# Hybrid decoder trunk: the order of the seven block products ahead of a norm, and the slot of the final norm's row

## The chip, the cores and the metric

The kernel runs on one core of one Trainium2 chip. The time is the device time of one execution in microseconds (us). All matrix products run on TensorE (PE), and the instructions of each engine run in the order in which a planner has put them.

## What is computed

The reference is two layers of a decoder trunk on 512 rows of 1024 numbers in float32. In each layer three branches (a state space scan, latent attention, a gated delta rule) read the normalised rows; their gated sum `mixed` passes through an output projection and a feed-forward block:

```python
xn = rmsnorm(x, norm1_g)
...
h = x + mixed @ w_out
f = jnp.square(jax.nn.relu(rmsnorm(h, norm2_g) @ w_up)) @ w_down
x = h + f
...
return rmsnorm(x, final_norm_g)
```

The change bears on `mixed @ w_out`, on `@ w_down`, and on the norms that follow them: `norm2` after the first, the next layer's `norm1` after the second in layer 0, the final norm after the second in layer 1.

## The kernel before

**Three matmuls for one.** Each float32 operand is split into a high and a low part (`split_half` L149 for weights, with the cast to `whi` on ScalarE, ACT, L154, and the difference `wlo` on VectorE, DVE, L155). `mm3` (L180) issues three matmuls, whose lines are L182, L183 and L184.

**Seven products for eight.** `seven` (L1123) multiplies a 512-row operand by a 1024 x 1024 block of weights with a scheme that forms sums of blocks first. The result has four quarters: row half i (rows 0 to 255 are half 0) and column half j. The seven products are named a11, a12, s1, s2, s3, s4 and a22; each is 24 matmuls, over four pieces of weights (k) and two row tiles (t). Their PSUM banks: `x` (two banks, one per row tile) gathers a11, then s2, s3 and a22 on top of it; `z` (two banks) takes s1, then s4 on top; a12 has banks of its own (`sm`). After each product its banks are added to, or subtracted from, a quarter of `h` by DVE (L1145): a11 and a12 make quarter (0,0), s2 and s4 make (0,1), s1 and s3 make (1,1), a22 makes (1,0). So half 0 is final after a12 and s4, half 1 after s3 and a22. Where a norm follows (`sq` is given), the sum of squares of each final piece is taken on ACT (L1147, L271), and a22 finishes row tile 0 before row tile 1.

The order of the seven products is written out by hand (L1163 to L1181): a11, a12, s2, s1, s3, s4, `before_last`, a22. Between them stand `plus4` (L1169, the weights of a22: DVE, two pieces) and the weights of s2, the two `halves`, which DVE adds at L1160 into slots of the pool tag "f".

**Three places use the hook `before_last`.** After `w_out` (both layers, L1255) it starts `norm2` for half 0 (`n2(0)`). After the last of the four blocks (`qd == 3`) of `w_down` in layer 0 it writes rows of half 0 to DRAM (`finish`, L1271) and starts the next layer's `norm1` for half 0. In layer 1 it does the final norm of half 0 and writes the output (L1268, L1269). `norm_half` (L279) adds the two sums of squares (L275), raises them to a power on GpSimd (L259), scales each row tile (DVE L285, 128x1024, into a tile of tag "f" or "xr"), transposes 16 blocks on PE into three `sm` banks, four blocks to a bank (L290), and splits each result into `xh` and `xl` (`split_gain`, ACT L254 and DVE L255). Half 1 follows inside the next projection, which works on half 0 alone first.

**Forms.** In the `w_out` product the left operands of the seven products are formed from `mixed` just ahead of each product (`forms` L1225, `form` L1230, by way of `pre`): a `comb` is one DVE instruction (L1217), a `put` one ACT (L1212) and one DVE instruction (L1213), each on 128x256 and four of them (d) to a product. In this order s2's step makes two combs and a put for each d, s1's step a put for s1, a comb and a put for s4. In the `w_down` products the operands are formed earlier, in `up`.

**What sets the order.** The planner simulates the kernel with a cost model of its own and puts on each engine, whenever that is free, the ready instruction of the highest priority; priority is the order of the program text, apart from blocks under `tc.high_priority()`. A pool tag has a fixed number of slots; a tile that asks for a slot waits until the earlier tile's readers are done. In `ends` (L1329) of layer 1 the row of the final norm `gb` asks for a slot of "f" (four slots, used just before by the four blocks f of `up`) and is loaded by DMA from SyncE's queue (SP), ahead of the two `halves` of `seven`.

Of the kernel before, what the change touches and what calls it, by code (L numbers as in the profile page):

```python
# [10 lines left out]
F32 = mybir.dt.float32  # L11
# [4 lines left out]
ALU = mybir.AluOpType  # L16
# [4 lines left out]
P = 128  # L21
S = 512
T = S // P
D = 1024
# [31 lines left out]
def hybrid_kernel(ctx, tc, a, out, depth=2, taps=None):  # L56
    nc = tc.nc
    pe, act, dve, pool, sync = nc.tensor, nc.scalar, nc.vector, nc.gpsimd, nc.sync
    uid = itertools.count()

    def mk(pl, shape, dt, tag, bufs=None):
        return pl.tile(shape, dt, tag=tag, name=f"{tag}_{next(uid)}", bufs=bufs)
# [269 lines left out]
    ssq = []  # L332
# [18 lines left out]
    for ly in range(depth):  # L351
# [198 lines left out]
        for hp in range(4):  # L550
# [37 lines left out]
            qd = mk(lp, [P, S], F32, "mix", 8)  # L588
# [29 lines left out]
            for j in range(2):  # L618
# [3 lines left out]
                for t in range(T):  # L622
# [10 lines left out]
                    n = (t + 1) * P  # L633
# [486 lines left out]

            return b, after

        def seven(pl, ops, b, sq=None, before_last=None, fin=None, nf=4, pre=None, mid=None):  # L1123

            x, z = ([acc_bank() for _ in range(2)] for _ in range(2))

            def product(ps, n, raw, start, i, j, op, done):

                w = []
                if pre:  # L1130
                    pre(n)
                for k in range(4):
                    w.append(split_half(raw(k)))
                    if done == 2 and sq:
                        continue
                    for t in range(2):
                        mul(ps, n, w, k, t, start)
                for t in range(2):
                    if done == 2 and sq:
                        for k in range(4):  # L1140
                            mul(ps, n, w, k, t, start)
                    r = 2 * i + t
                    hs_ = h[:, r, j * 512 : (j + 1) * 512]
                    with tc.high_priority():
                        dve.tensor_tensor(hs_, hs_, ps[t], op)  # L1145
                    if done and sq:
                        square(sq[r][:, j : j + 1], hs_, pl, "fs", 3 if nf == 4 else 2)  # L1147
                        if done == 2 and fin:
                            fin(r)

            def mul(ps, n, w, k, t, start):
                ah, al = (o[:, k % 2 * 256 + t * P : k % 2 * 256 + (t + 1) * P] for o in ops[n][k // 2])
                mm3(ps[t], ah, al, *w[k], start and k == 0, k == 3, not start)

            b11, p3, b21, b22, p1 = (b[n] for n in ((0, 0), (0, 1), (1, 0), (1, 1), "p1"))

            halves = [mk(pl, [P, 2 * S], F32, "f", nf) for _ in range(2)]
            for q, o in enumerate(halves):
                cs = slice(q * 1024, (q + 1) * 1024)
                dve.tensor_tensor(o, p1[:, cs], b22[:, cs], ALU.add)  # L1160
            p2 = lambda k: halves[k // 2][:, k % 2 * 512 : k % 2 * 512 + 512]
            of = lambda o: lambda k: o[:, k * 512 : (k + 1) * 512]
            product(x, "a11", of(b11), True, 0, 0, ALU.add, 0)  # L1163
            if mid:
                mid()
            product([sm_bank() for _ in range(2)], "a12", of(b21), True, 0, 0, ALU.add, 1)
            p4 = mk(pl, [P, 4 * 512], F32, "wr00") if mid else p1

            def plus4(q):  # L1169
                cs = slice(q * 1024, (q + 1) * 1024)  # L1170
                dve.tensor_tensor(p4[:, cs], halves[q], b21[:, cs], ALU.add)

            product(x, "s2", p2, False, 0, 1, ALU.subtract, 0)
            product(z, "s1", of(p1), True, 1, 1, ALU.add, 0)
            plus4(0)
            product(x, "s3", of(p3), False, 1, 1, ALU.subtract, 1)
            plus4(1)
            product(z, "s4", of(b22), False, 0, 1, ALU.add, 1)
            if before_last:
                before_last()  # L1180
            product(x, "a22", of(p4), False, 1, 0, ALU.add, 2)  # L1181

        with tc.tile_pool(name="wo", bufs=1, reuse_waits="tile") as wo:
            slots = {(1, 0): (wo, "wr11"), (1, 1): (hpl, "h"), (2, 0): (wo, "wr10"), (2, 1): (wo, "fs"),
                     (3, 0): (wo, "fs"), (3, 1): (wo, "fs")}

            def gate_tile(dp, j):
                pl, tag = slots[dp, j]
                return mk(pl, [P, S], F32, tag, 2 if tag == "fs" else 1)

            out_proj(a["w_gdn_out"][ly], 2, *yg, wo, (1, 2), make=gate_tile)
            h = mk(hpl, [P, T, D], F32, "h")
            for t in range(T):
                sync.dma_start(h[:, t, :], xsrc[t * P : (t + 1) * P, :])
            hts = [h[:, t] for t in range(T)]
            b, after = seven_weights(wo, a["w_out"][ly], 0)
            for c in range(4):
                after(c)
            ops = {}
            ck_pair = lambda: list(zip(*hilo_tags(lp, "ck", 2)))  # L1200
            ops["a11"], ops["s3"] = ck_pair(), list(zip(*hilo_tags(wo, "s3", 2)))

            def mid():
                out_proj(a["w_gdn_out"][ly], 2, *yg, wo, (3,), make=gate_tile, gate_banks=lambda: [sm_bank() for _ in range(2)])
                fh, fl = hilo_tags(lp, "x")
                for i, n in enumerate(("a12", "s2", "s1", "s4")):
                    ops[n] = [(fh[2 * i + e], fl[2 * i + e]) for e in range(2)]
                ops["a22"] = ck_pair()

            def put(n, d, s):  # L1210
                hi, lo = (x[:, d % 2 * 256 : d % 2 * 256 + 256] for x in ops[n][d // 2])
                act.mul(hi, s, 0.5)  # L1212
                dve.scalar_tensor_tensor(lo, s, 0.5, f32(hi), ALU.mult, ALU.subtract)  # L1213

            def comb(x, y, op):
                s = mk(wo, [P, 256], F32, "fc", 8)
                dve.tensor_tensor(s, x, y, op)  # L1217
                return s

            half = lambda i: lambda d: mixed[d][:, HALVES[i]]  # L1220
            t0, t1 = half(0), half(1)

            held = []

            def forms(n):  # L1225
                for d in range(4):
                    with tc.high_priority() if d > 1 and n in ("a12", "s2") else nullcontext():
                        form(n, d)

            def form(n, d):  # L1230
                if n == "a11":
                    put("a11", d, t0(d))
                    put("s3", d, comb(t0(d), t1(d), ALU.subtract))
                if n == "a12":
                    put("a12", d, t0(d + 4))
                if n == "s2":
                    s = comb(t1(d), t1(d + 4), ALU.subtract)
                    s2 = comb(s, t0(d), ALU.subtract)
                    put("s2", d, s2)
                    held.append((s, s2))  # L1240
                if n == "s1":
                    s, s2 = held[d]
                    put("s1", d, s)
                    put("s4", d, comb(t0(d + 4), s2, ALU.add))
                if n == "a22":
                    put("a22", d, t1(d + 4))

            nf = []

            def n2(i, pl, *tag):  # L1250
                if not nf:
                    nf.extend(hilo_tags(lp, "x"))
                norm_half(i, hts, ssq, lambda k: col(g_n2 + k), pl, *nf, *tag)

            seven(wo, ops, b, ssq, lambda: n2(0, wo, "f", 2), nf=2, pre=forms, mid=mid)  # L1255
            xh, xl = nf
        h_ssq = [mk(sp, [P, 2], F32, "nss", 4) for _ in range(T)]
        if not last:
# [14 lines left out]
        with tc.tile_pool(name="ff", bufs=1, reuse_waits="tile") as fp:  # L1273
# [55 lines left out]
            def ends(qd):  # L1329

                if qd < 3:
                    return None, None, None
                gb = None
                if last:
                    gb = mk(fp, [P, D], F32, "f", 4)
                    sync.dma_start(gb, a["final_norm_g"].partition_broadcast(P))
                fin = lambda r: finish(r, gb)

                def before_last():
                    for t in range(2):  # L1340
                        fin(t)
                    if not last:
                        norm_half(0, hts, h_ssq, lambda k: params[0][:, 124 + k : 125 + k], fp, *nx, "f", 4)

                return h_ssq, before_last, fin

            for qd in range(4):
                b, after = down_weights(qd)
                ops = up(qd, after)
                if qd == 3 and not last:  # L1350
                    nx = hilo_tags(lp, "x")
                seven(fp, ops, b, *ends(qd))
        if not last:
            xpl = h_pool.enter_context(tc.tile_pool(name="xp", bufs=1, reuse_waits="tile"))
            xt, ssq, xsrc = h, h_ssq, hd
# [39 lines left out]
```

## Time and profile before

| what | us |
|---|---|
| median of 3 runs | 2314.41 |
| lowest and highest of them | 2310.45 and 2318.05 |
| the profiled execution, its own time | 2314.88 |
| its span in the profile | 2313.1 |
| PE busy in the span | 2272.7 |
| DVE busy in the span | 1647.6 |
| ACT busy in the span | 1200.5 |

Times in the profile's rows count from the start of the span. A row of the timeline has the start, the duration, engine, line, operation, the tile written and the tiles read, the shape, the count of merged instructions, and in square brackets how long the engine stood idle ahead of it and whose end it waited for. PE's matmuls overlap one another and their ends are modelled, so the time from one start to the next says more of PE's pace than a duration.

### The profile page before, as it was taken

Reading aid. Unit: us, or ns where it says so; the run is one execution under the profiler, and the core shown is the slowest. Engines: PE = TensorE matmul, PEld = TensorE weight load, DVE = VectorE, ACT = ScalarE, POOL = GpSimd, SP = SyncE. Lnnn points to the kernel's source line nnn. Section 1 sums busy time; section 2 is a strip of 40 time slices with the busy share of each in tenths; the row PEclk is TensorE's granted clock in tenths of the full one; section 3 lists DMA queues with packets and bytes.
Section 4 is the critical chain, followed back from the end, with each engine's and each line's share of the span. In section 5 each row is a group of like instructions: output and inputs, shape, how many; then the busy total and the mean of one; then the engine's idle time right before and its main releaser. Section 6 shows DMA issues by size and latency. Waiting matters only on the chain.

```text
span 2313.1 us, 32290 instructions
## 1 busy us (share of the span) xinstructions
PE 2272.7 (98%) x11810; PEld 1866.7 (81%) x11810; DVE 1647.6 (71%) x3256; ACT 1200.5 (52%) x2509; POOL 59.5 (3%) x74
## 2 busy tenths in 40 slices
PE   9999999999999999999999999999999999999998
PEld 8788787878887888888888887878788878888886
DVE  7777566876667768767867775668657668778668
ACT  6766644333443455554657666433334435645545
POOL 0000000000000000000000000000000000000000
PEclk9999999999999999999999999999999999999999
DMA  4223534452324243233122236334422241433231
GB/s 142 80 74 101 191 101 119 125 140 74 87 69 164 65 146 107 94 104 108 59 89 79 75 107 197 95 112 141 119 82 83 65 164 55 160 107 101 89 110 46
DMA packets 220032, 244.16 MB, mean 106 GB/s; under 512 B 34256, under 2 KB 172384, under 8 KB 219872
## 3 DMA queue, kind: packets, MB, share of 16 engines
q1 hardware_dynamic: 219872, 242.09, 34.1%
q8 instruction: 93, 1.52, 0.3%
q14 instruction: 67, 0.55, 0.1%
HBM read 225.60 MB, written 11.74 MB: 103 GB/s over the span
## 4 chain that ended last, share of the span: by engine, by line
PE 86%; DVE 8%; ACT 2%; DMA 2%; POOL 1%; issue 1%; SPq 0%; DVEq 0%; POOLq 0%; ACTq 0%
PE acc L182 22%; PE acc L183 21%; PE acc L184 21%; PE sm L184 2%; PE sm L183 2%; PE sm L182 2%; DVE wlo L155 2%; PE sm L752 1%; ACT whi L154 1%; DVE tok L880 1%; PE sm L650 1%; DVE gQ L879 1%; PE sm L1037 1%; POOL gms L259 1%; PE yt L666 1%
## 5 line engine op out<-in xcount | busy, mean ns | idle before, releaser
L155 DVE TENSOR_TENSOR wlo<-wraw,whi 128x512 fp32r<-128x512 f32 (+1 forms) x536 | 366.4, 687 | 345.7 <-ACT whi L154 337.8
L154 ACT CAST whi<-wraw 128x512 fp32r<-128x512 f32 (+1 forms) x536 | 330.1, 618 | 541.5 <-PE acc L183 374.4
L182 PE MATMUL acc<-xh,whi 128*128 128x512 f32 (+1 forms) x1344 | 522.3, 390 | 0.8 <-ACT xh L254 0.8
L184 PE MATMUL acc<-xh,wlo 128*128 128x512 f32 (+1 forms) x1344 | 522.9, 389 | 0.0
L183 PE MATMUL acc<-xl,whi 128*128 128x512 f32 (+1 forms) x1344 | 522.2, 389 | 0.3 <-DVE xl L255 0.3
L183 PEld LDWEIGHTS acc<-xl,whi 128*128 128x128 f32 x1344 | 253.0, 188 | 48.7 <-DVE xl L255 1.4
L182 PEld LDWEIGHTS acc<-xh,whi 128*128 128x128 f32 x1344 | 252.4, 188 | 49.1 <-ACT xh L254 1.5
L184 PEld LDWEIGHTS acc<-xh,wlo 128*128 128x128 f32 x1344 | 253.0, 188 | 47.5
L154 ACT CAST whi<-wr 128x512 fp32r<-128x512 f32 x168 | 104.3, 621 | 108.7 <-PE acc L183 47.7
L183 PE MATMUL acc<-yl,whi 128*128 128x512 f32 x384 | 151.6, 395 | 0.0
L182 PE MATMUL acc<-yh,whi 128*128 128x512 f32 x384 | 150.9, 396 | 0.0
L184 PE MATMUL acc<-yh,wlo 128*128 128x512 f32 x384 | 150.1, 391 | 0.0
L155 DVE TENSOR_TENSOR wlo<-wr,whi 128x512 fp32r<-128x512 f32 x168 | 113.7, 689 | 38.1 <-ACT whi L154 37.4
L691 DVE SCALAR_TENSOR_TENSOR ckl<-acc,pc,ckl 128x511 f32<-128x511 f32 (+2 forms) x168 | 120.4, 744 | 15.5 <-ACT ckl L687 8.2
L182 PEld LDWEIGHTS acc<-yh,whi 128*128 128x128 f32 x384 | 71.7, 188 | 16.0 <-ACT yh L254 1.7
L184 PEld LDWEIGHTS acc<-yh,wlo 128*128 128x128 f32 x384 | 72.2, 188 | 14.5
L183 PEld LDWEIGHTS acc<-yl,whi 128*128 128x128 f32 x384 | 72.3, 188 | 13.8
L183 PE MATMUL acc<-wlo,xh 128*128 128x512 f32 (+1 forms) x208 | 80.1, 385 | 0.0
L184 PE MATMUL acc<-whi,xl 128*128 128x512 f32 (+1 forms) x208 | 79.7, 384 | 0.0
L182 PE MATMUL acc<-whi,xh 128*128 128x512 f32 (+1 forms) x208 | 79.2, 382 | 0.0
L1145 DVE TENSOR_TENSOR h<-h,acc 128x512 f32<-128x512 f32 x120 | 77.2, 682 | 0.2 <-PE acc L184 0.2
L454 ACT ACTIVATE eE<-eE,cum 128x128 f32<-128x128 f32 x192 | 63.1, 390 | 24.5 <-DMA eE<-d_c 19.8
(453 smaller groups left out, 4557.2 us busy)
## 6 DMA issues: line engine op xcount, KB each, us to landing
wraw<-in_w_in_dram SPq DMA_DIRECT2D x144, 512.0 KB, 3.6
wraw<-in_w_up_dram SPq DMA_DIRECT2D x64, 512.0 KB, 3.6
wr<-in_w_down_dram SPq DMA_DIRECT2D x32, 1024.0 KB, 5.5
eE<-d_c SPq DMA_DIRECT2D x48, 256.0 KB, 4.2
wraw<-in_w_mla_out_dram SPq DMA_DIRECT2D x16, 512.0 KB, 3.4
eE<-d_e SPq DMA_DIRECT2D x32, 256.0 KB, 2.9
wraw<-in_w_ssd_out_dram SPq DMA_DIRECT2D x16, 512.0 KB, 3.3
wraw<-in_w_gdn_out_dram SPq DMA_DIRECT2D x16, 512.0 KB, 3.3
```

The source lines that it names most:

```text
L154: act.copy(hi, raw)
L155: dve.tensor_tensor(lo, raw, f32(hi), ALU.subtract)
L182: pe.matmul(o, ah, bh, start=start, stop=False, skip_group_check=more)
L183: pe.matmul(o, ah, bl, start=False, stop=False, skip_group_check=more)
L184: pe.matmul(o, al, bh, start=False, stop=stop, skip_group_check=more)
L259: pool.tensor_tensor(o, o, (exp if exp is not None else nhalf)[:, : o.shape[1]], ALU.pow)
L454: act.activation(o[:, i], o[:, i], AF.Relu, scale=-1.0, bias=cum[:, t, h0 + i : h0 + i + 1])
L650: pe.transpose(ps[:, n : n + P], pn[t][:, kb * P : (kb + 1) * P], ident)
L666: pe.matmul(o, v_h, th[:, c : c + w], start=kb == 0, stop=False)
L691: dve.scalar_tensor_tensor(acc[:, d:], ps[:, : S - d], taps_[3 - d], acc[:, d:], ALU.mult, ALU.add)
L752: pe.matmul(py[64 * i : 64 * i + 64, c * P : (c + 1) * P], xd[:, t, h * 64 : (h + 1) * 64], e2[h // 4][:, h % 4, :], start=True, stop=True)
L1145: dve.tensor_tensor(hs_, hs_, ps[t], op)
```

## The change

In `seven` a flag `early` gives the order a11, a12, s1, s2, s4, s3, `before_last`, a22, so that half 0 is final after the fifth product. It is set for the `w_out` products of both layers and for the last `w_down` product of layer 0; the other products keep their order. The steps of `form` follow: s1's step now makes one comb and the put of s1, s2's step one comb and its put, s4's step one comb and its put, and the raised priority for d of 2 and 3 passes from s2 to s1. `plus4` follows s2 and s4 in the new order. In layer 1 the final norm's row is allocated and loaded in a hook `prep`, behind the two `halves`.

```diff
-        def seven(pl, ops, b, sq=None, before_last=None, fin=None, nf=4, pre=None, mid=None):
+        def seven(pl, ops, b, sq=None, before_last=None, fin=None, nf=4, pre=None, mid=None, prep=None, early=False):
...
                 dve.tensor_tensor(o, p1[:, cs], b22[:, cs], ALU.add)
+            if prep:
+                prep()
...
-            product(x, "s2", p2, False, 0, 1, ALU.subtract, 0)
-            product(z, "s1", of(p1), True, 1, 1, ALU.add, 0)
-            plus4(0)
-            product(x, "s3", of(p3), False, 1, 1, ALU.subtract, 1)
-            plus4(1)
-            product(z, "s4", of(b22), False, 0, 1, ALU.add, 1)
+            later = [lambda: plus4(0), lambda: plus4(1)]
+            for n in ("s1", "s2", "s4", "s3") if early else ("s2", "s1", "s3", "s4"):
+                if n == "s1":
+                    product(z, n, of(p1), True, 1, 1, ALU.add, 0)
+                if n == "s2":
+                    product(x, n, p2, False, 0, 1, ALU.subtract, 0)
+                if n == "s3":
+                    product(x, n, of(p3), False, 1, 1, ALU.subtract, 1)
+                if n == "s4":
+                    product(z, n, of(b22), False, 0, 1, ALU.add, 1)
+                if later and n in ("s2" if early else "s1", "s4" if early else "s3"):
+                    later.pop(0)()
...
-                    with tc.high_priority() if d > 1 and n in ("a12", "s2") else nullcontext():
+                    with tc.high_priority() if d > 1 and n in ("a12", "s1") else nullcontext():
...
+                if n == "s1":
+                    held.append(comb(t1(d), t1(d + 4), ALU.subtract))
+                    put("s1", d, held[d])
                 if n == "s2":
-                    s = comb(t1(d), t1(d + 4), ALU.subtract)
-                    s2 = comb(s, t0(d), ALU.subtract)
-                    put("s2", d, s2)
-                    held.append((s, s2))
-                if n == "s1":
-                    s, s2 = held[d]
-                    put("s1", d, s)
-                    put("s4", d, comb(t0(d + 4), s2, ALU.add))
+                    held[d] = comb(held[d], t0(d), ALU.subtract)
+                    put("s2", d, held[d])
+                if n == "s4":
+                    put("s4", d, comb(t0(d + 4), held[d], ALU.add))
...
-            seven(wo, ops, b, ssq, lambda: n2(0, wo, "f", 2), nf=2, pre=forms, mid=mid)
+            seven(wo, ops, b, ssq, lambda: n2(0, wo, "f", 2), nf=2, pre=forms, mid=mid, early=True)
...
-                gb = None
-                if last:
-                    gb = mk(fp, [P, D], F32, "f", 4)
-                    sync.dma_start(gb, a["final_norm_g"].partition_broadcast(P))
-                fin = lambda r: finish(r, gb)
+                gb = []
+
+                def prep():
+                    if last:
+                        gb.append(mk(fp, [P, D], F32, "f", 4))
+                        sync.dma_start(gb[0], a["final_norm_g"].partition_broadcast(P))
+
+                fin = lambda r: finish(r, gb and gb[0])
...
-                return h_ssq, before_last, fin
+                return dict(sq=h_ssq, before_last=before_last, fin=fin, prep=prep, early=not last)
...
-                seven(fp, ops, b, *ends(qd))
+                seven(fp, ops, b, **ends(qd))
```

More of the change, by code (lines that the diff above doesn't have):

```diff
@@ L1331, in ends @@
                 if qd < 3:
-                    return None, None, None
-                gb = None
-                if last:
-                    gb = mk(fp, [P, D], F32, "f", 4)
-                    sync.dma_start(gb, a["final_norm_g"].partition_broadcast(P))
-                fin = lambda r: finish(r, gb)
+                    return {}
+                gb = []
[4 more added lines that the diff above has]
+                fin = lambda r: finish(r, gb and gb[0])
                 def before_last():
```

## Prediction

> **What bounds the kernel now.** I read the page's busy times first, then the chain that ended last, then PE's busy time in the four stretches that the change touches.
>
> ```profile
> span 2313.1 us, 32290 instructions
> ...
> PE 2272.7 (98%) x11810; PEld 1866.7 (81%) x11810; DVE 1647.6 (71%) x3256; ACT 1200.5 (52%) x2509; POOL 59.5 (3%) x74
> ...
> PE 86%; DVE 8%; ACT 2%; DMA 2%; POOL 1%; issue 1%; SPq 0%; DVEq 0%; POOLq 0%; ACTq 0%
> ```
>
> PE is busy for 2272.7 of 2313.1 us and holds 86% of the chain: the kernel is as long as PE's stream of matmuls and its gaps. All gaps together are 40.4 us, so a change that adds and removes no matmul can win only from these, and only where it touches them.
>
> ```profile
> core 0: us, PE busy (x) PEld busy (x) DVE busy (x) ACT busy (x) POOL busy (x), PEclk, DMA share, GB/s
> 815.00:831.00 16.00, 14.17 (x89) 11.92 (x88) 13.20 (x30) 8.51 (x21) 2.48 (x4) 1.00 0.42 143
> 1150.00:1166.00 16.00, 14.97 (x86) 13.17 (x86) 12.51 (x30) 8.10 (x21) 3.04 (x6) 1.00 0.56 198
> 1961.00:1977.00 16.00, 14.18 (x88) 11.88 (x87) 13.33 (x30) 8.60 (x22) 2.48 (x4) 1.00 0.40 135
> 2270.00:2285.00 15.00, 13.71 (x60) 10.73 (x59) 14.09 (x22) 8.21 (x16) 0.00 (x0) 1.00 0.00 1
> ```
>
> The second column is the length of the stretch, the third PE's busy time in it. The first and third stretch are a22 and the norm behind `w_out` in the two layers: PE idles 1.83 and 1.82 us. The second is the same place behind `w_down` in layer 0: 1.03 us. The fourth holds the third product of the last `w_down` in layer 1: 1.29 us. That is 5.97 us of idle, about a seventh of all that PE has. The granted clock is 1.00 in all four, so they differ from the rest by waits alone.
>
> PE's timeline of the first stretch shows the waits one by one.
>
> ```profile
> 809.88 0.39 PE L182 MATMUL acc<-whi,xh 128*128 128x512 f32 x1
> ...
> 815.32 0.39 PE L182 MATMUL acc<-whi,ckh 128*128 128x512 f32 x1
> ...
> 818.29 0.40 PE L183 MATMUL acc<-wlo,ckh 128*128 128x512 f32 x1
> 819.09 0.55 PE L290 MATMUL sm<-ct,f 128*128 128x128 f32 x3 [0.40 <-DVE f L285]
> ...
> 820.41 1.15 PE L290 MATMUL sm<-ct,f 128*128 128x128 f32 x9
> ...
> 824.04 0.51 PE L182 MATMUL acc<-xh,whi 128*128 128x256 f32 x2 [0.38 <-ACT xh L254]
> 825.42 0.63 PE L290 MATMUL sm<-ct,f 128*128 128x128 f32 x4 [0.88 <-DVE xl L255]
> ...
> 829.95 0.39 PE L183 MATMUL acc<-xl,whi 128*128 128x256 f32 x1 [0.17 <-DVE xl L255]
> 831.25 1.47 PE L290 MATMUL sm<-ct,f 128*128 128x128 f32 x12
> ```
>
> s4 runs from 809.88 to 815.32, so a product of 24 matmuls takes 5.44 us and a matmul's slot 0.227 us. Then a22 starts, and the planner puts half 0's transposes (L290) into it, where it thought the scaled rows `f` ready; they came 0.40 us later, and the in-order PE waited with a22's matmuls behind. The rest follows from the same lateness: the up projection waits 0.38 us for `xh`, the fourth group of transposes 0.88 us for a bank that `split_gain` (L255) still reads, a last matmul 0.17 us for `xl`. From 818.29 to 819.09 are 0.80 us between starts where a slot is 0.227: this stall cost 0.57, not 0.40, as modelled ends hide a part. So idle time is a lower bound of the loss, and each stall hides up to 0.17 us more.
>
> ```profile
> 1154.11 0.55 PE L290 MATMUL sm<-ct,f 128*128 128x128 f32 x3 [0.50 <-DVE f L285]
> ...
> 1160.10 0.63 PE L290 MATMUL sm<-ct,f 128*128 128x128 f32 x4 [0.53 <-DVE xl L255]
> ```
>
> In layer 0's `w_down` these two are all of the 1.03 us.
>
> **The change part by part.** No matmul, transpose, split or DMA is added or removed in the three places: per `w_out` four combs of s1, four of s2, four of s4 and four puts each stay, only ordered otherwise. What counts is when they come.
>
> *Half 0 a product earlier.* The chain from s4's end to the scaled rows is read on DVE.
>
> ```profile
> 815.47 1.28 DVE L1145 TENSOR_TENSOR h<-h,acc 128x512 f32<-128x512 f32 x2
> ...
> 818.28 0.75 DVE L285 TENSOR_SCALAR f<-h,nrs 128x1024 f32<-128x1024 f32 x1 [0.32 <-POOL nrs L259]
> 818.95 0.68 DVE L1145 TENSOR_TENSOR h<-h,acc 128x512 f32<-128x512 f32 x1
> 819.55 0.75 DVE L285 TENSOR_SCALAR f<-h,nrs 128x1024 f32<-128x1024 f32 x1
> ```
>
> The first scaled tile is there at 819.03, 3.7 us after s4's end, the second at 820.30, 5.0 us after. With s3 between s4 and a22, a22 starts 5.44 us after s4's end, so both come 0.4 to 1.7 us ahead of it, even with the add at 818.95 in between, which moves away. What moves in are splits of s3's and a22's weights, high priority and 0.69 us each, two more than here; that can take the second tile to 0.3 us after a22's start, with eight transposes of the first tile to do until then. In program order the transposes stand behind all of s3, so PE takes them at the seam of s3 and a22, and the lateness of 0.40 that the planner didn't foresee falls into the margin. Then `xh` and `xl` of half 0 are made during a22's 5.44 us, and the waits of 0.38 and 0.17 in the up projection go too. Won: up to 1.83 and 1.82 us of idle in `w_out`, 1.03 in `w_down`.
>
> *What is late next.* Two things, which I price per place. First, s3 and a22 now follow each other on the same banks `x`. Before, z's or a12's product always stood between two products on a bank. a22's first matmul must wait until DVE has subtracted s3's result from `h`. In the rows above the seam is at 815.32, and the add of row tile 0 starts at 815.47 and takes 0.68 us (the single add at 818.95): it ends at 816.15, some 0.8 us after the seam. The 12 transposes that three banks hold take PE longer than that (1.15 us for 9, 1.47 for 12) and stand just there. With the cover it costs nothing, without it 0.8 us; I take 0.2. Second, the fourth group of transposes still waits for a bank of `sm`; it now falls into a22, where the planner again puts it by its own estimate. Between nothing and the 0.88 us of before I take 0.25. So 0.45 us per place stay, 1.35 in all.
>
> The Trainium skill speaks against this neighbourhood ("PSUM — Partial Sum Buffer", section "PSUM bank collisions raise a hardware error"): "Semaphore-guard PSUM by bank × quadrant". By that rule no matmul may enter `x` while DVE reads it, and no cover inside the bank is possible; the trace agrees so far that a bank's reader and PE never overlap in the rows above, and no run here shows the pair s3 and a22. Where the transposes stand elsewhere, this is the first rival below.
>
> *The forms.* DVE is nearly full when they are made.
>
> ```profile
> 785.00:805.00 20.00, 20.00 (x89) 16.22 (x88) 18.88 (x38) 12.71 (x29) 0.00 (x0) 1.00 0.01 2
> ...
> 807.36 0.42 DVE L1213 SCALAR_TENSOR_TENSOR xl<-fc,xh 128x256 fp32r<-128x256 f32 x1
> ```
>
> 18.88 of 20 us are busy, PE 20.00: DVE has just been fast enough. The row at 807.36 is the last low part of s4, done at 807.78. s4 now starts where s3 did, at 809.88 − 5.44 = 804.44, and needs it for its fourth piece of weights, three quarters of a product later, at 808.5. Even at the old pace that is 0.7 us early, and the third product's forms have become fewer (one comb instead of two). Cost: 0, bounded by the third rival's price.
>
> *The other moves.* `plus4` in `w_out` runs long before (its inputs are ready), in `w_down` beside PE. The write of half 0's rows to DRAM moves a product earlier on SP's queue:
>
> ```profile
> 1151.14 3.85 SPq L1271 DMA_DIRECT2D hd<-h  x3
> 1156.87 0.38 SPq L161 DMA_DIRECT2D wraw<-in_w_in_dram  x1
> ```
>
> The next load behind it comes at 1156.87 and has no earlier one to delay; cost 0. If that cover were gone, three issues within 3.85 us would be the most.
>
> *The final norm's row.* DVE's and SP's rows show the wait.
>
> ```profile
> 2259.11 0.34 SPq L1336 DMA_DIRECT2D f<-in_final_norm_g_dram  x1
> ...
> 2277.03 1.23 DVE L1160 TENSOR_TENSOR f<-wp,wr 128x1024 f32<-128x1024 f32 x1
> ...
> 2277.33 0.39 PE L184 MATMUL acc<-whi,mix 128*128 128x512 f32 x1
> 2279.01 0.73 PE L182 MATMUL acc<-whi,mix 128*128 128x512 f32 x2 [1.29 <-ACT whi L154]
> 2279.74 0.50 PE L183 MATMUL acc<-wlo,mix 128*128 128x512 f32 x1
> ...
> 2301.48 0.75 DVE L1268 SCALAR_TENSOR_TENSOR h<-h,nrs,f 128x512 f32<-128x512 f32 x1 [0.39 <-POOL nrs L259]
> ```
>
> The row took the slot that came free first; the second of the `halves` had to wait for a block f of the last part of `up` and ran at 2277.03 to 2278.26, in the middle of s2, which reads it. The cast behind it came late and PE lost 1.29 us of idle; by starts (1.68 − 0.227) + (0.73 − 0.454) = 1.73 us. In layer 0, where no such row is loaded, the same product is the control:
>
> ```profile
> 1116.05 2.35 DVE L1160 TENSOR_TENSOR f<-wp,wr 128x1024 f32<-128x1024 f32 x2
> ...
> 1116.00:1136.00 20.00, 20.00 (x90) 16.41 (x88) 19.26 (x32) 14.83 (x28) 0.00 (x0) 1.00 0.00 1
> ```
>
> Both halves are added together, ahead of a11, and PE is busy for 20.00 of 20 us. So this stall goes whole. The row's load then waits for the last blocks f, about 2275, and is first read at 2301.48, 26 us later, with an otherwise empty queue. PE's last matmul and the tail behind it move up with it.
>
> **The sum.** Idle removed: 1.83 + 1.82 + 1.03 + 1.29 = 5.97. Hidden by modelled ends: twelve stalls (four, four, two, two) at 0 to 0.17, I take 0.1: 1.2. Given back: 1.35. Net 5.97 + 1.2 − 1.35 = 5.8 us. From the profiled execution's 2314.88 that gives **2309.1 us**; against the median 2314.41, 0.5 us lower, it is 0.23% faster. The most that can go is 5.97 + 12 × 0.17 = 8.0; the least, with only the last term (1.29) and the seam uncovered three times (2.4), is a loss of 1.1.
>
> **The rivals.**
>
> *The wait is only moved.* The planner's transposes stand inside s3 or a22 instead of the seam, so that they wait again, and the seam waits for DVE. Then the three places win half: 1.29 + 0.4 for the last term, 2.3 for the others, near 2311. For it: the stalls of before come from a wrong estimate, which remains. Against: the margin of 0.4 to 1.7 us.
>
> *All goes, and more.* Less of ACT's and DVE's work falls into the up projection, half 1's chain is earlier too, nothing is given back: 8.0 us, 2306.9. For it: the waits form one chain with one cause.
>
> *DVE falls behind in `w_out`.* s4's forms stand a product earlier in a DVE that is busy for 18.88 of 20 us. If DVE is more than the 0.7 us late at s4's fourth piece, PE waits, and the norm behind gains nothing. Its price: if s4's four combs and four puts, eight instructions, have to run first, at 0.42 us less some overlap 3.0 us per `w_out`, 6.0 in all, against 0.9 (`w_down`) and 1.7 (final row) won: 2314.88 + 3.4 = 2318.3, slower than before. Against: PE has no idle time there now.
>
> *The order doesn't do what it says.* The norm's DVE work is queued behind s3's and a22's and half 0 comes no earlier; only the final row is won: 2313.2.
>
> **How the numbers follow.** The forecast has 0.50, the moved wait 0.22, the full gain 0.13, the late DVE 0.10, the order without effect 0.05. The three runs of before lie within 3.8 us of their median, so a new median may be some 2 us off by itself. From 8.0 us won and 2 us of spread below the median, 2304.4, to the least case, 2314.88 + 1.1 = 2316.0: that leaves out most of the late DVE and the tails. About 0.3% (6.9 us, 2307.5) is what a measurement of this kernel can tell from no change. The forecast lies 1.6 us short of it: a third of its case, three quarters of the full gain and a little of the first rival come out faster, 0.29; slower than 2321.4 only a part of the late DVE and strays, 0.05; the rest 0.66.
>
> **What would show it.** In the changed profile the transposes of half 0 stand between s3 and a22 in three places without an idle time ahead of them; the first up matmuls show no wait for `xh` or `xl`; L1160 runs twice together in layer 1's last block and PE is full in s2. Wrong would be an idle PE ahead of a22's first matmul with DVE's L1145 as releaser (the shared bank), waits of L184 for `xl` in s2 or s4 of `w_out` (the forms), or gaps elsewhere, because the planner's later order came out otherwise.

## The result, and the profile after

The changed kernel took 2308.73 us (median of 15 runs, 2306.11 to 2310.32) against 2314.57 us for the kernel before in the same rounds (15 runs, 2310.45 to 2319.77): 0.9974 of the time, with a 95% interval of 0.9968 to 0.9981. The forecast was 2309.1 us; the range 2304.4 to 2316.0 holds the time, and the 0.26% lie inside the 0.3% that were called no clear change, although the interval now excludes 1.

The page of the changed kernel answers to the three lines shown of before: span, busy times, chain by engine.

```profile
span 2308.2 us, 32276 instructions
...
PE 2272.9 (98%) x11810; PEld 1867.7 (81%) x11810; DVE 1645.9 (71%) x3256; ACT 1202.0 (52%) x2509; POOL 59.4 (3%) x74
...
PE 88%; DVE 6%; ACT 1%; DMA 1%; POOL 1%; issue 1%; SPq 0%; DVEq 0%; POOLq 0%; ACTq 0%
```

The same 11810 matmuls kept PE busy for 2272.9 us (2272.7 before); the gaps fell from 40.4 to 35.3 us, and PE's share of the chain rose to 88%.

Where they fell is read place by place. Each stretch begins at a11's first matmul. It ends, for `w_out`, at half 1's first transposes; for `w_down` of layer 0, at the first full-width matmul of the next layer's input projection; for the last block, at a22's first matmul. The view gives busy times by stretch: length and PE busy are the first two figures. The kernel before:

```profile
760.66:831.25 70.59, 68.76 (x329) 56.86 (x328) 56.34 (x112) 38.17 (x83) 2.48 (x4) 1.00 0.24 79
1117.54:1176.37 58.83, 57.80 (x297) 50.00 (x296) 48.53 (x93) 36.72 (x78) 4.09 (x8) 1.00 0.20 67
1906.92:1977.52 70.60, 68.78 (x330) 56.86 (x329) 56.39 (x112) 38.14 (x83) 2.48 (x4) 1.00 0.24 79
2263.96:2298.46 34.50, 33.21 (x146) 26.89 (x144) 29.26 (x45) 21.34 (x39) 0.00 (x0) 1.00 0.00 1
```

The changed kernel, between the same instructions:

```profile
763.42:832.92 69.50, 68.37 (x330) 56.65 (x329) 56.06 (x112) 38.45 (x83) 2.48 (x4) 1.00 0.20 66
1119.20:1177.14 57.94, 57.58 (x297) 50.28 (x296) 48.08 (x93) 36.99 (x78) 4.05 (x8) 1.00 0.19 68
1905.04:1974.47 69.43, 68.29 (x330) 56.63 (x328) 56.03 (x112) 38.46 (x83) 2.48 (x4) 1.00 0.20 66
2260.82:2293.58 32.76, 32.76 (x146) 26.95 (x145) 28.98 (x45) 21.19 (x39) 0.00 (x0) 1.00 0.05 17
```

Shorter by 1.09, 0.89, 1.17 and 1.74 us: 4.9 in all. In the last stretch PE has no idle time left; in the two of `w_out` it still idles 1.13 and 1.14 us. About two thirds of that is idle time that the kernel before did not have, as PE's timeline of the changed kernel shows for layer 0.

```profile
809.42 0.73 PE L182 MATMUL acc<-whi,s3h 128*128 128x512 f32 x2 [0.76 <-ACT whi L154]
...
819.24 0.27 PE L290 MATMUL sm<-ct,f 128*128 128x128 f32 x1
819.87 1.42 PE L290 MATMUL sm<-ct,f 128*128 128x128 f32 x11 [0.36 <-DVE f L285]
821.04 0.48 PE L182 MATMUL acc<-whi,ckh 128*128 128x512 f32 x1
...
824.13 0.60 PE L290 MATMUL sm<-ct,f 128*128 128x128 f32 x4
...
832.92 1.47 PE L290 MATMUL sm<-ct,f 128*128 128x128 f32 x12
```

The transposes of half 0 now stand between s3 and a22 (819.24 to 821.04), the fourth group (824.13) and the up projection wait for nothing, and the four stalls of before are down to one of 0.36 us. The prediction had asked for transposes without an idle time ahead of them; this 0.36 us remains. And at 809.42 PE has idled 0.76 us (0.92 by the starts), in s4, at a matmul of s3 that the planner has put ahead: a gap elsewhere, one of the signs of being wrong that the prediction named. DVE's rows there:

```profile
809.06 0.42 DVE L1225 TENSOR_TENSOR fc<-mix,fc 128x256 f32<-128x256 f32 x1
...
810.01 0.42 DVE L1221 SCALAR_TENSOR_TENSOR xl<-fc,xh 128x256 fp32r<-128x256 f32 x1
810.35 0.75 DVE L1225 TENSOR_TENSOR fc<-mix,fc 128x256 f32<-128x256 f32 x2
...
811.35 0.75 DVE L1221 SCALAR_TENSOR_TENSOR xl<-fc,xh 128x256 fp32r<-128x256 f32 x2
...
819.07 0.75 DVE L285 TENSOR_SCALAR f<-h,nrs 128x1024 f32<-128x1024 f32 x1
819.73 1.28 DVE L1145 TENSOR_TENSOR h<-h,acc 128x512 f32<-128x512 f32 x2
```

The last three forms of s4 (`fc`, then `xl`) run from 809.06 to 812.10, when s4, which began at 807.14, is already under way. In the last block DVE adds both halves together again, and the final norm's row is loaded later:

```profile
2259.34 2.35 DVE L1160 TENSOR_TENSOR f<-wp,wr 128x1024 f32<-128x1024 f32 x2
```
```profile
2270.44 0.34 SPq L1345 DMA_DIRECT2D f<-in_final_norm_g_dram  x1
```

### The profile page after: what moved, and what is told of

It reads as the page before. It is cut to its first block, busy times and chain, and to the rows that moved or that the text cites. A ratio compares the mean times of both kernels' runs of the same rounds, so it can differ in the third digit from the quotient of the medians.

```text
span 2308.2 us, 32276 instructions
## 1 busy us (share of the span) xinstructions
PE 2272.9 (98%) x11810; PEld 1867.7 (81%) x11810; DVE 1645.9 (71%) x3256; ACT 1202.0 (52%) x2509; POOL 59.4 (3%) x74
## 4 chain that ended last, share of the span: by engine, by line
PE 88%; DVE 6%; ACT 1%; DMA 1%; POOL 1%; issue 1%; SPq 0%; DVEq 0%; POOLq 0%; ACTq 0%
PE acc L182 22%; PE acc L183 22%; PE acc L184 22%; PE sm L182 3%; PE sm L184 3%; PE sm L183 3%; DVE wlo L155 2%; PE sm L752 1%; DVE tok L880 1%; PE sm L650 1%; DVE gQ L879 1%; PE sm L761 1%; PE sm L1037 1%; POOL gms L259 1%; ACT whi L154 1%
```

## The experiments

A single run of this kernel differs from the next by several us, but the stretches repeat within a tenth of one. So the runs are told apart by stretches, read as above between the starts of two PE rows. "Layer 0" and "layer 1" are longer ones, from a11 of `w_out` to a11 of the last `w_down` block.

| kernel | w_out, layer 0 | w_out, layer 1 | w_down, layer 0 | last block | layer 0 | layer 1 |
|---|---|---|---|---|---|---|
| before | 70.59 | 70.60 | 58.83 | 34.50 | 356.88 | 357.04 |
| changed | 69.50 | 69.43 | 57.94 | 32.76 | 355.78 | 355.78 |
| changed, again | 69.47 | 69.46 | 57.93 | 32.74 | 355.75 | 355.77 |
| row_only | 70.60 | 70.58 | 58.82 | 32.78 | 356.93 | 357.02 |
| w_out_only | 69.50 | 69.46 | 58.83 | 34.54 | 355.81 | 355.78 |
| row_twice | 70.56 | 70.59 | 60.55 | 34.54 | 356.87 | 356.95 |
| seam_bare | 70.19 | 70.17 | 57.95 | 32.75 | 356.44 | 356.43 |
| seam_plain | 69.51 | 69.43 | 57.91 | 32.75 | 358.63 | 358.56 |
| s4_prio | 68.82 | 68.78 | 57.97 | 32.74 | 355.22 | 355.10 |
| forms_less | 68.36 | 68.37 | 57.92 | 32.77 | 354.76 | 354.75 |
| scale_first | 69.55 | 69.58 | 57.91 | 32.77 | 355.90 | 355.97 |
| both_p | 68.81 | 68.78 | 57.89 | 32.77 | 355.19 | 355.17 |
| y_fourth | 69.55 | 69.55 | 57.67 | 32.76 | 355.27 | 355.16 |
| best | 68.84 | 68.85 | 57.03 | 32.77 | 354.50 | 354.58 |

My theory: PE's waits in the three places come from half 0's lateness and go with the earlier order; the last block's comes from the slot of the final norm's row. The rivals: the wait is only moved (to the seam of s3 and a22, or to the transposes), and DVE falls behind with s4's forms.

**The row alone.** The changed kernel with every order and form of before (shown is the line for `w_down`; `early` and the forms of `w_out` go back to the old order in the same way):

```diff
-                return dict(sq=h_ssq, before_last=before_last, fin=fin, prep=prep, early=not last)
+                return dict(sq=h_ssq, before_last=before_last, fin=fin, prep=prep, early=False)
```

> Only the final norm's row is allocated behind the halves; all seven products, their forms and hooks stand as before. Theory (the stall in s2 of the last block comes from the slot that the row took): the stretch from a11's first matmul to a22's first matmul in the last block falls from 34.50 us to 32.8 us, as in the changed kernel (32.76), and the other three places stay as before (70.6, 58.8 and 70.6 us). Rival (the stall belongs to the new order, or to chance): the stretch stays near 34.5 us.

The last block fell by 1.72 us, nothing else moved: the theory held. The opposite test gives layer 0's last block such a row as well, in the kernel before:

```diff
                 gb = None
+                if not last:
+                    dummy = mk(fp, [P, D], F32, "f", 4)
+                    sync.dma_start(dummy, a["final_norm_g"].partition_broadcast(P))
                 if last:
```

> The kernel before, with a second row loaded in layer 0's last w_down block as well, into the same pool and ahead of its halves; nothing reads it. Theory (the row's slot alone makes the stall): the second of the two adds that form the weights of s2 runs some 14 us later than the first in layer 0 too, and PE loses 1.5 to 1.9 us in s2 there; the stretch from a11 to the next projection's first full matmul goes from 58.8 to about 60.5 us. Rival (the stall in layer 1 comes from something else in the last block, the DMA or the output): layer 0 stays at 58.8 us.

`w_down` of layer 0 grew by 1.72 us. DVE's and PE's rows there:

```profile
1115.39 1.22 DVE L1160 TENSOR_TENSOR f<-wp,wr 128x1024 f32<-128x1024 f32 x1
1129.94 1.22 DVE L1160 TENSOR_TENSOR f<-wp,wr 128x1024 f32<-128x1024 f32 x1
```
```profile
1131.87 0.73 PE L182 MATMUL acc<-whi,mix 128*128 128x512 f32 x2 [1.24 <-ACT whi L154]
```

The second add runs 14.6 us after the first and PE stands in s2, as in layer 1 before the change. So the slot is the cause, and the two places where it was tried have the same price, 1.72 us.

**The order in `w_out` alone.** The row stands as before, and `early` is false for `w_down`.

> The new order and its forms only in the two w_out products; w_down and the final row as before. Theory (each place acts by itself): from a11's first matmul to half 1's first transposes 69.5 us in both layers (before 70.6), with the 0.92 us gap at the seam of s4 and s3 in both; w_down of layer 0 58.8 us and the last block 34.5 us as before. Rival (the gain in w_out needs the other edits, or the planner's order elsewhere changes with them): w_out at 70 us or more, or another place moved by over 0.3 us.

It gave the changed kernel's 69.5 us in both layers and left the other places as they were, as row_only had done for the last block. So these places add up; the new order in `w_down` of layer 0 had no run to itself.

**s4's forms.** First without them, which leaves s4's operand out of the computation (s4 uses s2's):

```diff
                 if n == "s4":
-                    put("s4", d, comb(t0(d + 4), held[d], ALU.add))
+                    pass
...
+                ops["s4"] = ops["s2"]
```

> The changed kernel without the forms of s4 in w_out: s4 multiplies by s2's operand, so that four combs and four puts per layer are left out. Theory (the gap at the seam of s4 and s3 is DVE's and ACT's work on s4's forms): the gap of 0.92 us is gone in both layers and w_out falls from 69.5 to 68.5 us or less, with the wait of the transposes for the second scaled tile smaller too. Rival (the gap is the weights' cast on ACT, which the row names as releaser): it stays, near 69.4 us.

The gap is gone and `w_out` is 1.1 us shorter. PE's rows behind it show all 12 first transposes in one group, with no wait listed:

```profile
818.71 1.57 PE L290 MATMUL sm<-ct,f 128*128 128x128 f32 x12
...
822.84 0.63 PE L290 MATMUL sm<-ct,f 128*128 128x128 f32 x4
```

So the releaser that the row at 809.42 names, a cast of weights on ACT, was the last link only. The order of instructions fits this: two matmuls of s3 stand ahead of s4's second piece (presumably because the planner found that piece not ready; its estimates are not on record), and they wait for a cast that itself waits for PE to free a slot of weights. The cause is s4's forms. The next run has the forms, at raised priority:

```diff
-                    with tc.high_priority() if d > 1 and n in ("a12", "s1") else nullcontext():
+                    with tc.high_priority() if d > 1 and n in ("a12", "s1") or n == "s4" else nullcontext():
```

> The changed kernel with the raised priority also for the forms of s4 in w_out. Theory (s4's forms are late because their place in the text moved from s1's step behind the whole of s2, and DVE runs the splits and adds first): the 0.92 us gap at the seam of s4 and s3 goes in both layers, from a11 to half 1's transposes 68.5 to 68.7 us instead of 69.5; 2 us of the whole, 2306.7 us median, 0.9965 of the kernel before. Rival (DVE has no room in that stretch, whoever goes first): the gap moves to s2 or s3 and the stretch stays at 69.3 us or more.

`w_out` fell by 0.68 and 0.65 us, less than the 0.8 to 1.0 expected. PE's rows in layer 0:

```profile
811.37 0.74 PE L184 MATMUL acc<-whi,xl 128*128 128x512 f32 x2 [0.32 <-DVE xl L1221]
...
822.40 1.42 PE L290 MATMUL sm<-ct,f 128*128 128x128 f32 x11 [0.15 <-DVE f L285]
```

s3's matmuls are back in their place, and what is left is a shorter wait for a low part itself. Theory and rival are each right in part: the place in the text costs about 0.65 us, and the rest of forms_less's 1.1 us is put down to DVE's room in that stretch, by subtraction alone. The run's median, 2309.99 us (0.9977, interval 0.9968 to 0.9986), missed the expected 2306.7 us and does not show 1.3 us; the kernel's differences between executions are larger.

**The seam of s3 and a22.** First I moved the hook behind a22:

```diff
-            if before_last:
+            if before_last and not early:
                 before_last()
             product(x, "a22", of(p4), False, 1, 0, ALU.add, 2)
+            if before_last and early:
+                before_last()
```

> The changed kernel, but before_last is called behind a22 in the three places with the new order, so that no transposes stand between s3 and a22. Theory (s3 and a22 share banks, and the transposes cover DVE's add): PE stands idle ahead of a22's first matmul in all three places, 0.6 to 1.0 us by the starts, with DVE's add to h (L1145) or an issue gap as releaser; and the norm of half 0 comes late, so that the projections behind wait some us. Rival (the add is quick enough or the pair isn't ordered by it): no gap over 0.2 us at that seam.

That did not lay the seam bare. The planner put five transposes into the hole all the same (six in `w_down`). `w_down` stayed at 57.95 us, and `w_out` lost 0.7 us. Its other transposes came behind a22, directly ahead of the up projection, which then started on fresh operands and lost time at some of its matmuls (in layer 0 at 831.38, one that reads `xl` starts 0.33 us after the one before, where a slot of this size is 0.12). The gap of 0.6 to 1.0 us was not to be seen. By the starts a22 came about 0.3 us late: 0.69 us after the start of a group of four transposes, which elsewhere take 0.36. DVE's add of row tile 0 had ended 0.15 us before. So the price is seen here only in part. The next run shows it whole: the new order in the blocks that have no norm behind them.

```diff
                 if qd < 3:
-                    return {}
+                    return dict(early=True)
```

> The changed kernel with the new order also in the other three w_down blocks of each layer, which have no norm behind them, so that a22 follows s3 on the same banks with nothing in between; all else as changed. Theory (a22 must wait for DVE's add of s3 out of the shared bank): a gap of 0.6 to 1.0 us by the starts ahead of a22 in all six blocks, released by DVE's add (L1145), 3.6 to 6 us of the whole; this is the price that the transposes hide at the three seams of the change. Rival (PE does not wait there, and the transposes hide nothing): no gap over 0.2 us in the six blocks.

Layer 0 and layer 1 grew by 2.85 and 2.78 us for three blocks each. PE's rows at one of layer 0's seams, and DVE's and ACT's beside it:

```profile
985.92 0.39 PE L184 MATMUL acc<-whi,mix 128*128 128x512 f32 x1
987.08 0.47 PE L182 MATMUL acc<-whi,yh 128*128 128x512 f32 x1 [0.77 <-ACT whi L154]
```
```profile
986.25 1.28 DVE L1145 TENSOR_TENSOR h<-h,acc 128x512 f32<-128x512 f32 x2
```
```profile
982.26 0.62 ACT L154 CAST whi<-wp 128x512 fp32r<-128x512 f32 x1 [0.74 <-PE acc L184]
...
986.34 0.62 ACT L154 CAST whi<-wp 128x512 fp32r<-128x512 f32 x1 [0.73 <-DVE wlo L155]
```

By the starts the gap is 987.08 − 985.92 − 0.227 = 0.93 us. The row names an ACT cast, but a22's first piece was cast at 982.26; the one that ends at 986.96 is its fourth. a22's first matmul waits for semaphores of DVE and ACT, and what ends just ahead of it is DVE's add of row tile 0, from 986.25 to 986.93. All six seams have the same gap. That the cast isn't the reason can be seen in the kernel before, at the same place, where s4 stands ahead of a22 and the banks differ. There a22's first matmul starts before the fourth cast does:

```profile
986.88 0.39 PE L182 MATMUL acc<-whi,yh 128*128 128x512 f32 x1
```
```profile
987.08 0.63 ACT L154 CAST whi<-wp 128x512 fp32r<-128x512 f32 x1 [0.73 <-DVE wlo L155]
```

This is the case of a wait for several semaphores put down to the wrong one.

**The scaled tile ahead of a split.** PE's last wait at the seam is for the second scaled tile, which stands behind a split on DVE:

```diff
-            dve.tensor_scalar(xr[-1], xs[t], rs, None, ALU.mult)
+            with tc.high_priority() if i == 0 else nullcontext(): dve.tensor_scalar(xr[-1], xs[t], rs, None, ALU.mult)
```

> The changed kernel with the scaling of half 0's row tiles (L285) at raised priority: on DVE it changes places with one split of weights, PE's order is the same. Theory (PE waits at the seam for the second scaled tile, which stood behind a split of 0.69 us): the wait of 0.36 to 0.38 us ahead of the transposes goes in all three places, 1.2 us of the whole, and the split that is now later starves nothing. Rival (the split is on the path): a wait of the same size appears at a22's matmuls for wlo, no gain.

The order on PE was the same, the second tile came 0.4 to 0.5 us sooner, and nothing was won. PE's rows in layer 0:

```profile
818.87 1.63 PE L290 MATMUL sm<-ct,f 128*128 128x128 f32 x12
...
823.84 0.63 PE L290 MATMUL sm<-ct,f 128*128 128x128 f32 x4 [0.25 <-DVE xl L255]
```

The wait ahead of the first group is gone and one ahead of the fourth has come (0.41 us by the starts): the fourth group needs a bank that the first group's `split_gain` must free, and DVE is no further with that. In `w_down` the wait ahead of the first group is gone too, and the fourth group starts 0.52 us after the matmul before it, 0.29 more than a slot. Neither theory had this. Then both edits together:

> Both of these edits together. If they are independent: w_out 68.1 to 68.3 us per layer instead of 69.5, w_down of layer 0 57.5 instead of 57.9, 3.2 us of the whole, 2305.5 us median, 0.996 of the kernel before. If the forms at raised priority push the chain of the norm back: no better than the better of the two.

The stretches are no better than the better edit's: 68.8 us as in s4_prio, 57.89 us as in scale_first. But this is no second test of the bank. In `w_out` the order of instructions on PE, DVE and ACT is that of s4_prio: with s4's forms first, the two scaled tiles follow each other on DVE already, and the second edit has nothing left to move there. The wait of 0.15 us for the second tile stays, and the fourth group waits for nothing. By time it is 2308.35 us (2305.5 had been expected if the two were independent), 0.9963 of the kernel before (0.9951 to 0.9976), beside the changed kernel on the same chip:

> The changed kernel once more, on the chip of the two others: 2308.7 us, 0.9974 of the kernel before, and the same gaps at the same seams (0.92 us in w_out, 0.40 us at the transposes).

It took 2308.14 us, 0.9964 (0.9951 to 0.9978).

**A bank for the fourth group.** The bank `yt` is free at that time:

```diff
-            ps = sm_bank()
+            ps = y_bank() if k == 6 else sm_bank()
```

> The changed kernel with the fourth group of a norm's transposes in the bank yt, which is free then, instead of the third sm bank's second use. Theory (the fourth group waits for split_gain to free a bank and breaks into a22): all 16 transposes stand together at the seam, the second break in a22 goes, 0.1 to 0.4 us per place. Rival (DVE's chain, not the bank, is what PE waits for): no gain over 0.1 us in w_out or w_down.

`w_down` won 0.27 us and the two layers 0.5 and 0.6; in `w_out` the stretch ends ahead of half 1's transposes and shows nothing. The gain of the layers lies behind that, where half 1's fourth group now follows on the other three and no longer breaks into the up projection. With all three edits:

> s4's forms at raised priority, the row scaling ahead of the split, and the fourth group in the bank yt, together. If each removes its wait: w_out 68.3 us per layer instead of 69.5, w_down of layer 0 57.4 instead of 57.9, 2.9 us of the whole, 0.9988 of the changed kernel. If DVE's work in that stretch is the bound: 68.8 and 57.9 as with the forms' priority alone.

At the seams PE's rows show all 16 transposes in one go, first in `w_out` of layer 0, then in `w_down`:

```profile
821.88 1.84 PE L290 MATMUL sm<-ct,f 128*128 128x128 f32 x12
823.55 0.60 PE L290 MATMUL yt<-ct,f 128*128 128x128 f32 x4
...
1153.77 1.47 PE L290 MATMUL sm<-ct,f 128*128 128x128 f32 x12
1155.08 0.60 PE L290 MATMUL yt<-ct,f 128*128 128x128 f32 x4
```

In `w_down` the 12 take 1.31 us from start to start and wait for nothing. In `w_out` they take 1.67: PE still waits there for the second scaled tile, and the merged row hides it (in layer 1 the same place is listed with 0.15 us of idle time).

The layers fell by another 1.28 and 1.20 us and `w_down` by 0.91: 3.4 us below the changed kernel in all. `w_out`, at 68.8 us, is as in s4_prio, the second of the two expectations; `w_down`, at 57.03, is better than either had it. There the edits are not independent: scale_first alone won 0.03 us and y_fourth 0.27, together 0.91. So the scaled tile's wait pays off only once the fourth group has its own bank. By time it is 2308.39 us against 2318.75 of before on its chip, 0.9956 (0.9940 to 0.9972); this interval overlaps the changed kernel's, so that the runs' times alone do not part the two.

## Why the prediction was right, and where a term was off

*The last block:* 1.29 + 0.2 = 1.49 us in the sum, 1.74 measured, 1.72 by row_only, and row_twice shows the slot as cause. The prediction's own reading by the starts, 1.73, was right; the sum left it for the idle time plus 0.1 for each of two stalls, although this one stall hid 0.44. *`w_down` of layer 0:* 1.03 + 0.2 − 0.45 = 0.78 forecast, 0.89 measured. *`w_out`:* 1.83 + 0.4 − 0.45 = 1.78 per layer forecast, 1.09 and 1.17 measured. The sum, 5.8 us, compares with 4.9 by places; that the medians differ by 5.84, almost exactly the forecast, is in part luck, as their interval (0.19% to 0.32%, 4.4 to 7.4 us) is wide.

*The failed step is the forms' cost of 0.* I took the old pace of s4's last low part, 807.78, against a deadline of 808.5. But in the old text s4's forms belonged to s1's step, and in the new one they stand in a step of their own behind all of s2: their place in the order of priorities went back while their deadline came forward. In the changed trace they end at 812.10, which is 809.34 counted from before's start of a11 (2.76 us less). And the deadline that counted was not the last piece's but the second's: its low part (810.01) ended at 810.43, when s4's first six matmuls had started by 808.27. s4_prio shows the place in the text as a cause worth 0.68 and 0.65 us, forms_less the forms as a whole as one worth 1.14 and 1.06. The third rival's mechanism was right with a smaller price: 0.92 + 0.12 us in layer 0, not 3.0 per layer. The forms came late one after another beside PE's work, not all ahead of it. DVE's 18.88 of 20 us was the warning.

*The seam* was priced at 0.8 us uncovered and measured at 0.93; in the change the transposes cover it (821.04 follows on them with no idle time listed, and the add of row tile 0 has ended at 820.41). By the Trainium skill ("PSUM — Partial Sum Buffer", section "PSUM bank collisions raise a hardware error") a bank's reader and writer must be kept apart with semaphores. The traces agree: in seam_plain a22's first matmul starts at 987.08, behind the add's end at 986.93. They don't test that rule, as a22 must wait here for its result's sake as well. seam_plain gives the time that this takes when nothing stands in the hole: 0.93 us.

*The margin of the scaled tiles* came out narrower than worked out: first tile 818.54, second 819.82 against a seam at 819.24. The first was 0.7 us early instead of 1.7, the second 0.6 us late instead of 0.3. I had counted on eight transposes of the first tile to fill that; the planner put one. The wait of 0.36 to 0.38 us was within the 0.45 given back per place, but that had been meant for other things: 0.2 for the bank at the seam, and 0.25 for the fourth group, which waited for nothing until scale_first removed the first wait.

*The first rival* (the wait moved, 4.0 us won) had its condition unmet, as the transposes do stand at the seam; the 4.9 us by places lie midway between it and the forecast. *All goes, and more* (8.0 us) and *the order without effect* fell with the first trace.

## What to carry to other kernels

When a step is moved ahead, move everything it needs by as much, and look up where those instructions stand in the order of priorities, not only when they used to end: here an operand's forms went back in that order, and `w_out` won over a third less than forecast. A wait that is removed in a chain with one busy engine shows up at the next link; test the pair, since each edit alone may show little (in `w_down` 0.03 and 0.27 us alone, 0.91 together), and see in the trace that both edits still move something. Where single executions differ by more than the effect, compare stretches between the same instructions of two traces, with untouched stretches as control.

## What the runs showed beyond that

The stretch from the start to a11 of `w_out` in layer 0 has the same order of instructions on PE in the kernel before, the changed kernel, row_only, w_out_only, row_twice, seam_bare, seam_plain, s4_prio and forms_less. It took from 760.00 us (row_twice, mean granted clock 0.998) to 766.71 us (s4_prio, 0.996). The three shortest had clocks of 0.998 to 0.999, the three longest 0.996, so the clock goes along with it; a clock lower by 0.2% to 0.3% makes at most 2.3 us of these 6.7, and the rest stays unexplained. The stretches of the table, in the same traces, agree within 0.1 us wherever the kernels have the same edits.
